# Gate 1 and shift 2 summed on VectorE during the scan, scale 2 and gate 2 on TensorE during convolution and gate

## The chip, the cores and the metric

The kernel runs on one core of a Trainium2 chip. The metric is the device time of one execution in microseconds (us); lower is better. Engines: PE is TensorE (PEld its weight loads), DVE is VectorE, ACT is ScalarE, POOL is GpSimd, SP is SyncE, whose queue issues nearly all transfers. Each engine works through its own instructions in a fixed order and waits for others by semaphores.

## The reference, cut to what matters

One layer works on 256 latent tokens `x` and 256 context tokens `ctx`, each 1024 wide. Six modulation vectors of 1024 come from the conditioning vector `c`:

```python
mod_x = (jax.nn.silu(c) @ w_mod[i] + b_mod[i]).reshape(b, N_MOD, 1, D_MODEL)
...
hx = modulate(rmsnorm(x, norm1_g[i]), mod_x[:, 0], mod_x[:, 1])
ox, _, _ = token_mixers(hx, *mix_w, conv_grid_cols, h0_f, h0_b)
x = x + mod_x[:, 2] * ox
x = x + mod_x[:, 5] * moe(modulate(rmsnorm(x, norm2_g[i]), mod_x[:, 3], mod_x[:, 4]), *moe_w)
return rmsnorm(x, final_g)
```

Vectors 0 and 1 (shift 1, scale 1) are wanted at once and are not touched here. Vector 2 (**gate 1**) is wanted after the out-projection, vectors 3 and 4 (**shift 2**, **scale 2**) ahead of the router, vector 5 (**gate 2**) in the mixture of experts. Each pair is a product of one row of 1024 with a 1024 x 2048 block of `w_mod` (8 MB), plus a bias.

`token_mixers` is an in-projection, a depthwise convolution, a bidirectional state-space scan over 16 heads, a second short convolution over three more slices of the projection (B, C, U), a SiLU gate z and an out-projection. `moe` is a top-4-of-32 mixture of experts, whose weights are some 400 MB.

## The kernel before

**Stages.** The program runs, in this order: modulation of shift 1 and scale 1 with the first projections; the decays (`token_steps`, `decay_rows`) and the x columns (`x_block`, `x_tokens`); the scan of 16 steps (`decays(s)`, then `outputs(s)`), in which blocks of the short convolution (`sc_block`) fill TensorE; the other 12 convolution blocks; eight gate blocks (`proj` of Z); the out-projection, in eight parts; the router; the experts.

**Order.** From L405 on, PE's order is that of the program text (`manual_schedule` for PE). The other engines' instructions and the transfers on SP's queue are put in order by a planner when the kernel is built; `tc.issue_after(i)` makes an instruction stand behind `i` on the same engine.

**The modulation products before.** `mods(1, ...)` is gate 1 with shift 2, `mods(2, ...)` scale 2 with gate 2. Each is a generator: eight steps k, and a last part. A step loads 1 MB of `w_mod` (`load_mod`, L187; two ring slots, `ringm`, so that step k+2 is loaded when step k has been read) and issues four matmuls (L202) of a 32-column stationary operand `ct[:, k, :]`, which the trace shows as eight. After step 7 the bias is added on DVE (L205). The last part (L209 to L218) turns one vector into columns (`pq`, 16 records) and spreads the other over all partitions (`pgate`, four records).

**Where the steps stand.** Three steps of `m1` stand between `c_block(0)` and `token_steps` (L649), two after `scores(1)` (L669), one in each scan step from 2 on (L679): `m1` to the end in steps 2 to 5, then `m2`, whose last part falls into step 14. One scan step before is: a convolution block of 24 matmuls, one step of `mods`, the decay matmuls `rb` of the next scan step, and the products `py` of this one. `decays` also makes six exponentials on ACT, two products `mx` on DVE (L586) and two `ex` on POOL (L588); `outputs` needs them one scan step later.

**Buffers the prediction speaks of.** `sacc` is one tile that `rows` of `m1`, `rows` of `m2` and then `bgr` (the rounded expert biases, L861 and L862) use in turn. The ring slot of `bg`, which `bgr` is made from, is later used by one of the eight loads `wo` of the out-projection. `proj` and `misc` are pairs of PSUM buffers. `hi` and `lo` (L287, L288) are the two parts into which each weight block is split, on ACT and on DVE or POOL.

Of the kernel before, what the change touches and what calls it, by code (L numbers as in the profile page):

```python
# [8 lines left out]
F32 = mybir.dt.float32  # L9
# [5 lines left out]
ALU = mybir.AluOpType  # L15
# [3 lines left out]
P = 128  # L19
D = 1024  # L20
KD = D // P
# [41 lines left out]
def body(ctx, tc, x, ctx_in, vectors_in, w_mod, b_mod, w_in, w_out, w_router, b_router, w_gate_up, b_gate_up,  # L63
         w_down, b_down, final_g, out, taps=None):
    nc = tc.nc
# [126 lines left out]
    def mods(ph, gate, gate_first, col):  # L192

        acc = ps.tile([P, 512], F32, tag="pm", bufs=1, name=f"pmod{ph}")
        rows = mp.tile([P, 512], F32, tag="sacc", name=f"rows{ph}")
        nc.gpsimd.memset(rows, 0.0)
        nc.gpsimd.dma_start(rows.rearrange("(j p) n -> j p n", p=32)[:, 0, :],
                            dram(b_mod, ph * 2048, [[512, 4], [1, 512]]))
        for k in range(KD):
            w = load_mod(ph, k)  # L200
            for j in range(4):
                nc.tensor.matmul(acc[32 * j:32 * j + 32, :], ct[:, k, :], w[:, 512 * j:512 * j + 512],  # L202
                                 start=(k == 0), stop=(k == KD - 1), skip_group_check=True)
            if k == KD - 1:
                nc.vector.tensor_add(rows, rows, acc)  # L205
            yield
        jg, jc = (0, 2) if gate_first else (2, 0)
        pq = ps.tile([P, 512], F32, tag="misc", bufs=2, name=f"pq{ph}")
        for q in range(KD):  # L209
            j = jc + q // 4  # L210
            nc.tensor.matmul(pq[:, q:q + 1], rows[:, (q % 4) * P:(q % 4 + 1) * P], ident[:, 32 * j:32 * j + 1],
                             start=True, stop=True)
        nc.vector.tensor_copy(col, pq[:, 0:KD])
        for hf in range(2):
            j = jg + hf
            pg = ps.tile([P, 512], F32, tag="misc", bufs=2, name=f"pgate{ph}_{hf}")
            nc.tensor.matmul(pg, ident[:, 32 * j:32 * j + 1].to_broadcast([P, P]), rows, start=True, stop=True)
            nc.scalar.copy(gate[:, hf, :], pg)  # L218
        yield

# [256 lines left out]
    sh2 = cn.tile([P, 8], F32, name="sh2")  # L477
    g1 = mp.tile([P, 2, 512], F32, tag="g1", name="g1")
    g2 = mp.tile([P, 2, 512], F32, name="g2")
    m1 = mods(1, g1, True, sh2)  # L480
    m2 = mods(2, g2, False, gs2)
    yb = mp.tile([P, 8, T], F32, tag="x28", name="yb")
    ws = t2a.tile([P, 2, NT, NH, HD], F32, tag="big8", name="ws")
# [66 lines left out]
    cb = [None, None]  # L550
# [14 lines left out]
    def decays(s_):  # L565

        hp, d_ = s_ // 2, s_ % 2
        g = hp // 4
        ja, jb = (0, 1) if d_ == 0 else (1, 0)
        mxs, exs = [], []  # L570
        for h_ in (2 * hp, 2 * hp + 1):
            row = 32 * d_ + h_
            pr = ps.tile([P, 4, P], F32, tag="rb", bufs=2, name=f"rb{h_}_{d_}")
            nc.tensor.matmul(pr, selr[:, row:row + 1].to_broadcast([P, P]), a4, start=True, stop=False,
                             skip_group_check=True)
            for blk in (0, 2) if d_ == 0 else (1, 2):
                nc.tensor.matmul(pr[:, blk, :], identb, maskf if d_ == 0 else maskb, start=False,
                                 stop=(blk == 2), skip_group_check=True)
            mx = t2s.tile([P, 384], F32, tag="mx", bufs=4, name=f"mx{h_}_{d_}")
            with tc.issue_after(last_silu):  # L580
                nc.scalar.activation(mx[:, 0:256], pr[:, 0:2, :].rearrange("p a b -> p (a b)"), AF.Exp,
                                     bias=dtc[:, 2, ja, row:row + 1])
                nc.scalar.activation(mx[:, 256:384], pr[:, 2, :], AF.Exp, bias=dtc[:, 2, jb, row:row + 1])
                ex = t2s.tile([P, 2, P], F32, tag="ex", bufs=4, name=f"ex{h_}_{d_}")
                nc.scalar.activation(ex, pr[:, 3:0:-2, :] if d_ == 0 else pr[:, 0:4:3, :], AF.Exp)
            nc.vector.tensor_mul(mx, mx, cb[g][d_])  # L586
            exf = ex.rearrange("p a b -> p (a b)")
            nc.gpsimd.tensor_tensor(exf, exf, cch[g], op=ALU.mult)  # L588
            mxs.append(mx)
            exs.append(exf)  # L590
        return mxs, exs
# [3 lines left out]
    def outputs(s_, mxs, exs):  # L595
        hp, d_ = s_ // 2, s_ % 2
        g = hp // 4
        ja, jb = (0, 1) if d_ == 0 else (1, 0)
        half = slice(P, T) if d_ == 0 else slice(0, P)
        xd = xdt[:, d_]  # L600
        if d_ == 0:
            py[0] = ps.tile([P, T], F32, tag="py", bufs=1, name=f"py{hp}")
        for hh in range(2):
            nc.tensor.matmul(py[0][64 * hh:64 * hh + 64, :], xd[:, ja, 2 * hp + hh, :], mxs[hh][:, 0:256],
                             start=(d_ == 0), stop=False, skip_group_check=True)
        for hh in range(2):
            nc.tensor.matmul(py[0][64 * hh:64 * hh + 64, half], xd[:, jb, 2 * hp + hh, :], mxs[hh][:, 256:384],
                             start=False, stop=False, skip_group_check=True)
        for hh in range(2):
            h_ = 2 * hp + hh  # L610
            nc.tensor.matmul(py[0][64 * hh:64 * hh + 64, :], h0[d_][g][:, (h_ % 8) * HD:(h_ % 8 + 1) * HD], exs[hh],
                             start=False, stop=(d_ == 1), skip_group_check=True)
        if d_ == 1:
            nc.vector.tensor_add(yb[:, hp, :], yb[:, hp, :], py[0])
# [31 lines left out]
    context_b(1)  # L646
    x_block(3)
    c_block(0)
    for _ in range(3):  # L649
        next(m1)  # L650
    token_steps()
    x_tokens(0)
    x_tokens(1)
# [12 lines left out]
    last_silu = x_block(7)  # L666
    x_tokens(6)
    scores(1)
    for _ in range(2):  # L669
        next(m1)  # L670
    x_tokens(7)
    sc_steps = [(kind, 2 * q + half) for q in range(4) for kind in "CUB" for half in range(2)]
    fill = [lambda: context_state(0, 1), lambda: context_state(1, 1)]
# [2 lines left out]
    for s_ in range(16):  # L676
        if fill:
            fill.pop(0)()
        if s_ >= 2:  # L679
            next(m1 if s_ < 6 else m2, None)  # L680
        done_ = step
        if s_ < 15:
            step = decays(s_ + 1)
        outputs(s_, *done_)
    tap("y", yb)
    sa.close()
# [8 lines left out]
    def sc_parts():  # L695
        while sc_done:
            ti, v_ = sc_done.pop(0)
            nc.scalar.copy(sc[0][:, ti, :], v_)
            nc.gpsimd.tensor_tensor(sc[1][:, ti, :], v_, sc[0][:, ti, :].bitcast(F32), op=ALU.subtract)

    sc_parts()
    for a in sc_steps[12:]:
        sc_block(*a)
        sc_parts()


    yhl = [scp.tile([P, 2, 4, T], F32R, tag=("ya", "yb")[g], name=f"y{g}") for g in range(2)]
# [56 lines left out]
    for q in range(4):  # L764
        if q == 3:
            wo0, slot0 = load_out(0), ring[-1]
            ahead = [row_parts(wo0, 0, hf, order[0]) for hf in range(2)]
        wv = load_cols(256 * q, f"Z{q}")
        for half in range(2):
            ti = 2 * q + half  # L770
            pp = proj(wv, half, T, f"Z{ti}", nc.vector)
            z = t2b.tile([P, T], F32, tag="cv1", bufs=6, name=f"z{ti}")
            nc.scalar.activation(z, pp[:, :T], AF.Silu)
            nc.vector.tensor_mul(yb[:, ti, :], yb[:, ti, :], z)
# [703 lines left out]
```

## Time and profile before

| | |
|---|---|
| median of 3 runs | 1302.51 us (1299.98 to 1302.81) |
| the profiled execution | 1297.97 us, of which the span is 1296.2 us |
| mean granted clock of TensorE | 0.97 of full speed |
| busy share of the span | PE 90%, DVE 34%, ACT 20%, POOL 9% |
| moved | 466.12 MB, mean 360 GB/s |

The span is the time from the first to the last instruction of the profiled execution; the 1.8 us beside it lie outside. Busy shares are averages over stages with different limits, so a stage has to be read by itself. A matmul's duration in a list of instructions overlaps its neighbours'; what a run of matmuls costs is read from the chain of work that ended last, or from the distance of two starts.

### The profile page before, as it was taken

Reading aid. Unit: us, or ns where it says so; the run is one execution under the profiler, and the core shown is the slowest. Engines: PE = TensorE matmul, PEld = TensorE weight load, DVE = VectorE, ACT = ScalarE, POOL = GpSimd, SP = SyncE. Lnnn points to the kernel's source line nnn. Section 1 sums busy time; section 2 is a strip of 40 time slices with the busy share of each in tenths; the row PEclk is TensorE's granted clock in tenths of the full one; section 3 lists DMA queues with packets and bytes.
Section 4 is the critical chain, followed back from the end, with each engine's and each line's share of the span. In section 5 each row is a group of like instructions: output and inputs, shape, how many; then the busy total and the mean of one; then the engine's idle time right before and its main releaser. Section 6 shows DMA issues by size and latency. Waiting matters only on the chain.

```text
span 1296.2 us, 16117 instructions
## 1 busy us (share of the span) xinstructions
PE 1170.4 (90%) x6113; PEld 538.1 (42%) x6113; DVE 435.6 (34%) x878; ACT 258.4 (20%) x510; POOL 122.1 (9%) x140
## 2 busy tenths in 40 slices
PE   7989999999899989899898878998977899888985
PEld 6666767988433322243222223422321243223221
DVE  5475454654432432213324212222321113212222
ACT  5444544554400010010001001000100010001002
POOL 1232333426100100000000000000000000000000
PEclk9999999999899999999999989999998999899998
DMA  9743468786499999999999999999999999999994
GB/s 324 266 164 130 164 228 280 257 294 270 170 417 415 416 415 417 416 416 417 417 416 416 416 416 416 416 416 416 416 416 417 417 416 417 416 416 416 416 415 186
DMA packets 111841, 466.12 MB, mean 360 GB/s; under 512 B 9576, under 2 KB 40424, under 8 KB 76944
## 3 DMA queue, kind: packets, MB, share of 16 engines
q1 hardware_dynamic: 111504, 464.37, 90.4%
q8 instruction: 50, 0.82, 0.3%
q0 software_dynamic: 256, 0.67, 0.1%
q14 instruction: 31, 0.25, 0.1%
HBM read 463.97 MB, written 1.05 MB: 359 GB/s over the span
## 4 chain that ended last, share of the span: by engine, by line
PE 77%; DMA 13%; DVE 6%; ACT 2%; issue 1%; SPq 1%; POOL 0%; ACTq 0%; DVEq 0%; POOLq 0%
PE pdn L1123 8%; PE pg L1111 8%; DMA gu<-in_w_gate_up_dram 8%; PE pl L1111 7%; PE pg L1191 6%; PE pc L1087 6%; PE pgl L1160 6%; PE pdn L1175 4%; PE pdn L1198 3%; DMA dn<-in_w_down_dram 3%; PE pd L999 2%; DMA wim<-in_w_mod_dram 2%; PE pgl L1154 1%; PE pat L1080 1%; PE ppX L293 1%; PE ppX L294 1%
## 5 line engine op out<-in xcount | busy, mean ns | idle before, releaser
L1111 PE MATMUL pg<-gu,xe 128*64 128x512 f32 x480 | 152.6, 610 | 1.5 <-DMA gu<-in_w_gate_up_dram 1.5
L1111 PE MATMUL pl<-gu,xe 128*64 128x512 f32 x480 | 149.3, 599 | 0.0
L1054 ACT ACTIVATE s<-a 128x512 f32<-128x512 f32 (+1 forms) x35 | 19.1, 545 | 591.0 <-DVE a L1053 591.0
L1087 PE MATMUL pc<-ye,gt 64*128 64x512 f32 (+1 forms) x248 | 100.3, 647 | 27.6 <-DVE ye L1134 14.5
L1160 PE MATMUL pgl<-gu,xe 128*32 128x512 f32 x896 | 114.4, 617 | 11.8 <-DMA gu<-in_w_gate_up_dram 11.8
L1123 PE MATMUL pdn<-dn,at 128*64 128x512 f32 x480 | 117.3, 634 | 6.9 <-ACT at L1082 6.8
L1089 DVE TENSOR_TENSOR x<-x,pc 128x512 f32<-128x512 f32 x124 | 81.7, 684 | 123.1 <-PE pc L1087 123.1
L1053 DVE TENSOR_SCALAR a<-pg 128x512 f32<-128x512 f32 x21 | 14.5, 690 | 216.0 <-PE pg L1111 150.5
L1191 PE MATMUL pg<-gu,xe 128*128 128x512 f32 x192 | 83.9, 592 | 0.0
L1134 DVE TENSOR_TENSOR ye<-g2s,pdn 128x512 f32<-128x512 f32 x29 | 19.9, 687 | 153.1 <-PE pdn L1123 106.3
L1313 POOL DMA_DIRECT2D fg<-in_final_g_dram x1 | 0.6, 591 | 746.4 <-PE pd L999 746.4
L1087 PEld LDWEIGHTS pc<-ye,gt 64*128 64x128 f32 (+1 forms) x248 | 28.5, 186 | 100.5 <-DVE x L1089 42.9
L1111 PEld LDWEIGHTS pl<-gu,xe 128*64 128x64 f32 x480 | 42.2, 138 | 67.1 <-issue 66.8
L1175 PE MATMUL pdn<-dn,at 128*32 128x512 f32 x448 | 63.4, 674 | 6.5 <-ACT at L1082 5.4
L1111 PEld LDWEIGHTS pg<-gu,xe 128*64 128x64 f32 x480 | 38.5, 138 | 69.9 <-issue 60.1
L1123 PEld LDWEIGHTS pdn<-dn,at 128*64 128x64 f32 x480 | 33.9, 145 | 72.8 <-issue 58.0
L1160 PEld LDWEIGHTS pgl<-gu,xe 128*32 128x32 f32 x896 | 24.9, 111 | 88.4 <-issue 56.7
L1191 PEld LDWEIGHTS pg<-gu,xe 128*128 128x128 f32 x192 | 35.8, 190 | 41.6 <-issue 40.9
L999 PE MATMUL pd<-oh,hr 128*128 128x256 f32 (+1 forms) x256 | 41.9, 305 | 5.6 <-DVE xe L1001 5.0
L1198 PE MATMUL pdn<-dn,at 128*128 128x512 f32 x96 | 43.5, 601 | 0.0
L999 PEld LDWEIGHTS pd<-oh,hr 128*128 128x128 f32 x256 | 34.2, 198 | 20.9 <-DVE xe L1001 10.7
L1067 DVE TENSOR_SCALAR go<-io,gp 128x128 f32<-128x128 f32 x56 | 18.6, 369 | 67.0 <-PE pgo L1071 67.0
(406 smaller groups left out, 1635.0 us busy)
## 6 DMA issues: line engine op xcount, KB each, us to landing
gu<-in_w_gate_up_dram SPq DMA_DIRECT2D x256, 1024.0 KB, 19.9
dn<-in_w_down_dram SPq DMA_DIRECT2D x127, 1024.0 KB, 20.0
wm<-in_w_mod_dram SPq DMA_DIRECT2D x16, 1024.0 KB, 5.2
wim<-in_w_mod_dram SPq DMA_DIRECT2D x8, 1024.0 KB, 11.6
wo<-in_w_out_dram SPq DMA_DIRECT2D x8, 1024.0 KB, 5.1
wiX<-in_w_in_dram SPq DMA_DIRECT2D x4, 1024.0 KB, 9.9
wiSC<-in_w_in_dram SPq DMA_DIRECT2D x4, 1024.0 KB, 6.4
wiSU<-in_w_in_dram SPq DMA_DIRECT2D x4, 1024.0 KB, 6.5
```

The lines of the kernel that those rows point to most:

```text
L999: nc.tensor.matmul(pd[:, :width], hr[n // 2][:, n % 2, k * P:(k + 1) * P], oh[:, n % 2, :], start=(n == 0), stop=(n == 3))
L1054: nc.scalar.activation(s, a, AF.Sigmoid, scale=ALPHA)
L1067: nc.vector.tensor_scalar(go if cap == P else go.rearrange("p (a s) -> p a s", s=cap), io1 if cap == P else io1[:, None, 0:cap].to_broadca ...
L1087: nc.tensor.matmul(pc_, lhs, rhs, start=True, stop=True)
L1089: return nc.vector.tensor_add(ysl, ysl, pc_).ins
L1111: nc.tensor.matmul(pp[64 * hf:64 * hf + 64, :], xk[k], gu[k][:, i * FF + hf * 512:i * FF + hf * 512 + 512], start=False, stop=(k == KD - 1 ...
L1123: down = nc.tensor.matmul(pdn[64 * hf:64 * hf + 64, :], at[:, kk % 4, 64 * (kk // 4):64 * (kk // 4) + 64], dn[kk // 2][:, (kk % 2) * D + h ...
L1134: nc.vector.tensor_mul(ye, g2s, pdn)
L1160: nc.tensor.matmul(pgl[32 * q:32 * q + 32, :], xk[k], gv[:, :, 256 * q:256 * q + 256], start=False, stop=(k == KD - 1), skip_group_check=True)
L1175: down = nc.tensor.matmul(pdn[j:j + 32, :], at[:, c2, 32 * q:32 * q + 32], dn[q][:, c2 * D + hf * 512:c2 * D + hf * 512 + 512], start=(q = ...
L1191: nc.tensor.matmul(pgs[i][hf], xk[k], gu[k][:, i * FF + hf * 512:i * FF + hf * 512 + 512], start=False, stop=(k == KD - 1))
L1198: nc.tensor.matmul(pdn, ats[kk // 4][:, kk % 4, :], dn[kk // 2][:, (kk % 2) * D + hf * 512:(kk % 2) * D + hf * 512 + 512], start=(kk == 0) ...
```

## The change

`m1` is made by a new generator, `mods_by_rows`; `m2` stays as it was. For each k, `mods_by_rows` multiplies the two halves of the loaded 128 x 2048 block by the per-partition scalar `ct[:, k, 0:1]` and adds them to two accumulators of 128 x 1024 (`gate`, `sacc`) with `scalar_tensor_tensor` on DVE: two instructions in a step, 16 in all, each pair ordered behind the last `mx` product that the program text has issued. GpSimd clears the accumulators and loads the biases into their first rows. The last part sums over the partitions with matmuls against ones: eight for the columns of shift 2, two for gate 1.

The places move: the three early steps and the two after `scores(1)` are gone; a step of `m1` stands in each odd scan step (1, 3, ... 15), behind `decays`; the last part of `m1` stands behind the first of the 12 later convolution blocks, steps 0 to 2 of `m2` behind the fourth, seventh and tenth, steps 3 to 7 behind the matmuls of gate blocks 0 to 4, and the last part of `m2` behind those of gate block 5.

```diff
+    scanned = [None]
+
+    def mods_by_rows(ph, gate, gate_first, col):
+        sacc = mp.tile([P, 2, 512], F32, tag="sacc", name=f"sacc{ph}")
+        parts = (gate, sacc) if gate_first else (sacc, gate)
+        for h_, a in enumerate(parts):
+            nc.gpsimd.memset(a, 0.0)
+            nc.gpsimd.dma_start(a[0:1], dram(b_mod, ph * 2048 + h_ * 1024, [[0, 1], [512, 2], [1, 512]]))
+        for k in range(KD):
+            w = load_mod(ph, k)
+            with tc.issue_after(scanned[0]):
+                for j in range(2):
+                    a = parts[j].rearrange("p a n -> p (a n)")
+                    nc.vector.scalar_tensor_tensor(a, w[:, D * j:D * j + D], ct[:, k, 0:1], a,
+                                                   op0=ALU.mult, op1=ALU.add)
+            yield
+        pq = ps.tile([P, 512], F32, tag="misc", bufs=2, name=f"pq{ph}")
+        for q in range(KD):
+            nc.tensor.matmul(pq[:, q:q + 1], sacc[:, q // 4, (q % 4) * P:(q % 4 + 1) * P], onesf[:, 0:1],
+                             start=True, stop=True)
+        nc.vector.tensor_copy(col, pq[:, 0:KD])
+        for hf in range(2):
+            pg = ps.tile([P, 512], F32, tag="misc", bufs=2, name=f"pgate{ph}_{hf}")
+            nc.tensor.matmul(pg, onesf, gate[:, hf, :], start=True, stop=True)
+            nc.scalar.copy(gate[:, hf, :], pg)
+        yield
...
-    m1 = mods(1, g1, True, sh2)
+    m1 = mods_by_rows(1, g1, True, sh2)
...
-            nc.vector.tensor_mul(mx, mx, cb[g][d_])
+            scanned[0] = nc.vector.tensor_mul(mx, mx, cb[g][d_]).ins
...
     c_block(0)
-    for _ in range(3):
-        next(m1)
     token_steps()
...
     scores(1)
-    for _ in range(2):
-        next(m1)
     x_tokens(7)
...
-        if s_ >= 2:
-            next(m1 if s_ < 6 else m2, None)
         done_ = step
         if s_ < 15:
             step = decays(s_ + 1)
+        if s_ % 2:
+            next(m1)
         outputs(s_, *done_)
...
-    for a in sc_steps[12:]:
+    for i_, a in enumerate(sc_steps[12:]):
         sc_block(*a)
         sc_parts()
+        if i_ % 3 == 0:
+            next(m2 if i_ else m1)
...
             pp = proj(wv, half, T, f"Z{ti}", nc.vector)
+            if ti < 6:
+                next(m2)
```

## Rows read from the trace of the kernel before

**Rows 1.** The page, part 2: GB/s moved in 40 slices of the span.

```profile
GB/s 324 266 164 130 164 228 280 257 294 270 170 417 415 416 415 417 416 416 417 417 416 416 416 416 416 416 416 416 416 416 417 417 416 417 416 416 416 416 415 186
```

**Rows 2.** Stretches: length, busy PE, PEld, DVE, ACT, POOL; granted clock, DMA share, GB/s.

```profile
75.57:83.83 8.26, 3.87 (x26) 0.69 (x26) 8.04 (x18) 3.94 (x5) 3.47 (x2) 0.88 0.70 256
...
131.84:217.26 85.42, 85.06 (x665) 59.25 (x663) 43.80 (x67) 42.27 (x104) 32.12 (x36) 1.00 0.66 221
...
217.26:251.86 34.60, 34.60 (x289) 34.60 (x289) 20.25 (x29) 15.77 (x21) 13.14 (x10) 1.00 0.78 254
251.86:274.94 23.08, 23.08 (x194) 23.08 (x193) 12.85 (x17) 11.64 (x17) 2.65 (x2) 1.00 0.70 237
274.94:321.90 46.96, 46.28 (x218) 37.90 (x217) 21.68 (x40) 24.50 (x48) 27.79 (x25) 1.00 0.79 311
321.90:346.00 24.10, 18.75 (x100) 12.33 (x100) 17.49 (x47) 12.66 (x32) 6.29 (x5) 0.86 0.27 102
400.00:1280.00 880.00, 786.62 (x3672) 266.22 (x3672) 227.60 (x456) 74.38 (x160) 5.58 (x5) 0.97 1.01 414
```

**Rows 3.** Waits of PE, whole span: us in total, times, longest.

```profile
PE pmod L202 <- DMA wm<-in_w_mod_dram: 4.4, 1, 4.4
...
PE px L519 <- DVE ws L522: 1.0, 1, 1.0
```

**Rows 4.** The chain that ended last, 70 to 90 us: start, us, what.

```profile
75.64 1.04 PE pmod L202 x8
...
76.70 5.14 DMA wm<-in_w_mod_dram
...
83.82 0.83 PE pc L470 x6
...
86.09 0.12 PE ppC L293
```

**Rows 5.** DVE's instructions in order of time, around 80 us.

```profile
76.44 0.40 DVE L460 TENSOR_TENSOR wc<-wc,dtx 64x256 f32<-64x256 f32 x1
...
79.52 3.25 DVE L288 TENSOR_TENSOR loC<-wiC,hiC 128x1024 fp32r<-128x1024 f32 x1
82.69 0.73 DVE L312 SCALAR_TENSOR_TENSOR cv<-ppX,vs,cv 128x510 f32<-128x510 f32 x1
```

**Rows 6.** ACT's instructions in order of time, around 79 us.

```profile
78.97 0.77 ACT L311 ACTIVATE cv<-ppX,vs 128x512 f32<-128x512 f32 x1
```

**Rows 7.** POOL's instructions in order of time, around 79 us.

```profile
79.23 2.46 POOL L288 TENSOR_TENSOR loX<-wiX,hiX 128x1024 fp32r<-128x1024 f32 x1
```

**Rows 8.** The chain that ended last, in the scan: start, us, what.

```profile
174.90 1.00 PE pmod L202 x8
...
176.86 0.58 PE py L604 x4
...
209.43 1.88 PE pq L211 x16
211.30 1.84 PE pgate L217 x4
...
215.31 0.67 DVE mx L586
```

**Rows 9.** Groups by form, 131.84 to 217.26 us: busy us, mean ns.

```profile
L202 PE MATMUL pmod<-wm,ct 128*32 128x512 f32 x88 | 11.7, 605 | 0.0
...
L288 DVE TENSOR_TENSOR loSC<-wiSC,hiSC 128x1024 fp32r<-128x1024 f32 x4 | 4.9, 1218 | 0.0
```

**Rows 10.** DVE's instructions in order of time, in the scan.

```profile
172.24 1.11 DVE L586 TENSOR_TENSOR mx<-mx,cbf 128x384 f32<-128x384 f32 x1
```

**Rows 11.** Groups by form, 60 to 80 us: busy us, mean ns.

```profile
L438 DVE SCALAR_TENSOR_TENSOR e<-e,e 64x512 f32<-64x512 f32 x1 | 0.7, 682 | 0.0
```

**Rows 12.** The tile of the `w_mod` loads: time from issue to landing.

```profile
DMA to landing us min/median/max: 4.7/5.2/8.4
```

**Rows 13.** Waits of SP's own queue.

```profile
SPq L751 <- DVE bgr L862: 2.4, 1, 2.4
```

## The prediction

> **What bounds the kernel now.** I read the page's slices first: from the twelfth on, the transfers run at 415 to 417 GB/s up to the last one [rows 1], and from 400 to 1280 us the share of the transfer engines is 1.01 [rows 2]. The experts are bound by transfers; the stretch ahead of them only decides when that stream can start. Its start is set by the first ring slot that the first expert gives back, for ahead of it the transfers stand idle: their share is 0.27 between 321.90 and 346 us, because every slot is full [rows 2]. So what the change saves or costs before the first expert moves the end by as much, as long as the slots are still full by then.
>
> The second view is busy time by stage [rows 2]. In the scan (131.84 to 217.26 us) PE works 85.06 of 85.42 us, in convolution and gate (to 274.94) all of the time. There each microsecond put on PE or taken off it counts in full. The one stretch where it doesn't is 75.57 to 83.83 us: PE 3.87 of 8.26 us, DVE 8.04.
>
> The third view is PE's waits: the longest in this part is the 4.4 us for the third `wm` block; later there is 1.0 us for `ws` [rows 3]. The scan has none worth naming. So the change lives or dies by how much PE work really disappears, and by whether DVE, which gets new work, makes PE wait.
>
> **Part 1: what only moves.** `m2`'s eight steps (1.00 us each [rows 8]) and its last part (1.88 + 1.84 = 3.72 us [rows 8]) go from the scan to convolution and gate, both full on PE: 0. The last part of `m1` moves likewise and keeps its size (eight column products and two of 512 columns with a 128-row operand, as before): 0. In all about 15.4 us leave the scan and come back behind it.
>
> **Part 2: three steps of `m1` that leave the scan.** 88 records [rows 9] are 11 steps of eight, eight of `m2` and three of `m1`: -3.0 us.
>
> **Part 3: three steps ahead of `token_steps`.** From the first `pmod` at 75.64 to `pc` at 83.82 are 8.2 us: two steps, the 5.14 us transfer that could only start when a slot was read, and the third step [rows 4]. But `pc` also needs `wc`, which DVE has only at 76.84 [rows 5], so 6.9 us at most come free. Nor can PE run on for all of that: the next projection, `ppC` at 86.09 [rows 4], needs the PSUM buffer that X block 3's two `cv` instructions on DVE release. ACT's part of it ended at 79.74 [rows 6], and with two instructions of 0.73 us [rows 5] DVE could release it at 81.2: 4.9 us sooner, less some 0.4 of hand-over, so -4.5 at best. If DVE keeps its order, with `loC` ahead of `cv` (79.52, 82.69 [rows 5]), it is released at 84.2: -1.5. DVE is full here [rows 2], and the `dtc`, `xdt` and `ws` work now competes with it earlier. I take the middle: -3.0 us, between -4.5 and -1.5.
>
> **Part 4: two steps after `scores(1)`.** PE does them and then still waits 1.0 us for `ws` [rows 3]. Without them it waits 2 us longer: 0, at best -1.9 us if DVE is put in another order.
>
> **Part 5: what DVE gets.** 16 instructions over 1024 columns. One of 512 columns with two SBUF inputs takes 0.68 us [rows 11], `loSC`, a two-input instruction of 1024, takes 1.22 [rows 9]; I take 1.22, so a pair is 2.44 us and the eight are 19.5 us. Do they fit? Without the `pmod`s the stretch of 85.42 us shrinks by 11.0 + 3.5 + 3.7 = 18.2 to 67.2 us; DVE's 43.8 us [rows 2], less 1.6 us of `rows` and small copies, plus seven pairs in it are 59.3: 88%. The delay allowed: the second `mx` of a step ended at 173.35 [rows 10], and its `py` starts at 176.86 [rows 8], 1.0 us sooner without `pmod`: 2.5 us of slack against a pair of 2.44, which moreover stands behind that `mx`, not ahead of it. Queued behind a pair are `lo`, `cs` and `scv` (who wait for two blocks yet) and the next `mx`. So in full steps I charge 0. At the end it is tighter: steps 14 and 15 have no convolution block, and the 3.72 us of `m2`'s last part covered the last `mx`, which ended at 215.98, 2.8 us after that part [rows 8]. Of the 3.72 us part will turn into waiting, and a pair may stand ahead of the last `mx`. Bounds 0 and 3.7; I take +1.5, since `rb` and `py` fill about half of it.
>
> **Part 6: transfers.** `m1`'s blocks are read every second scan step, so a slot is free some 21 us before its next use: 0. In the gate, steps 5 to 7 of `m2` need a block whose slot was freed two gate blocks before: 2 x (2.88 + 1.00) - 1.0 = 6.8 us (2.88 is 23.08 us over eight blocks [rows 2]). Landing took 4.7 to 8.4 us, median 5.2 [rows 12]: 0 at the median, 3 x 1.6 at the worst, and the share of the transfer engines there was 0.70 [rows 2]: +0.7, up to 4.8. A wait is added on SP too: a `wo` load waits for `bgr` [rows 13], which now waits for `sacc`, free only after gate block 5. Behind it on SP stand the later `wo` loads and the first expert blocks, some 5 MB and 2 MB late. The out-projection wants that `wo` about 15 us later, and idle share (0.21 of 47 us and 0.73 of 24 us, 27 us [rows 2]) holds the 18 us that 7 MB take at 400 GB/s. With `bgr`'s instructions falling into busier time: +0.3, up to 1.5.
>
> **The sum.** -3.0 (scan) - 3.0 (early) + 0 + 1.5 (tail) + 0.7 + 0.3 = -3.5 us. The profiled execution would go from 1297.97 to 1294.5 us; it lies 4.5 us under the median of the runs shown, so against that median I forecast 1302.5 - 3.5 = 1299.0 us. The ends: -3.0 - 4.5 - 1.9 = -9.4 (1293.1), and -3.0 - 1.5 + 3.7 + 4.8 + 1.5 = +5.5 (1308.0), the latter only if all three losses come together. A measurement of this kernel can tell about 0.2%, 2.6 us, from no change.
>
> **Rivals.**
> *No difference.* The early gain stays at its lower end and the late losses are middling: -3.0 - 1.5 + 2.5 + 1.5 + 0.5 = 0, 1302.5 us. For it speaks that DVE, not PE, is the full engine where the wait is removed. Or the loads of the gate come late: +4.8 in place of 0.7 is +0.6, 1303.1 us. Together 0.30.
>
> *Slower: PE waits for `mx` behind the pairs.* The planner may put a pair ahead of the next step's `mx`, and a pair need not take 2.44 us: `loC` took 3.25 us in place of 1.22 while POOL ran `loX` to 81.69 [rows 5, 7], and the `ex` products and `scv` run on POOL in every such step. The slack of 2.5 us is what decides: above it each further delay is PE's. If each of seven pairs overruns by one instruction, 1.22 us, that is +8.5: 1307.5 us. Against it: it has to happen in most steps, and average DVE load leaves 12%. 0.14.
>
> *Slower: the new instructions run at half rate.* Two SBUF inputs might be read in turns; then a pair is 2 x (0.15 + 2 x 1.07) = 4.6 us (1.07 us being 1024 columns at the step of 1.05 ns between 0.68 us at 512 and 1.22 at 1024 [rows 9, 11]), seven are 32 us, DVE has 74 us of work in 67, and the sum is -3.5 + 6.9 = +3.4: 1305.9 us. Against it: the 0.68 us instruction is just such a one and shows no second reading. The Trainium skill has this as a rule (Vector Engine (DVE) Microarchitecture Reference, "Points that are easy to get wrong"): a scalar-tensor-tensor instruction with two SBUF sources that aren't bf16 halves its throughput. The trace so far doesn't bear that out. 0.05.
>
> *The change doesn't do what it says.* The planner puts pairs off, past the scan, so that the last part of `m1` waits on PE behind the first convolution block: two pairs late are +4.9, 1303.9 to 1307 us. `issue_after` holds only one side of the order. 0.03.
>
> **How the numbers follow.** The forecast with its better variants (the early stretch at -4.5, the tail at 0) has 0.48; it needs the early gain to be over its lower end, which I can't see from here. No difference 0.30, slower 0.22. Its own range is 1293 to 1300. The range leaves out the end below 1293.5 and part of the slower cases, 0.05 and 0.13: 1293.5 to 1306.5.
>
> **What would show it.** In the trace after: no `pmod` before the scan, and `pc` near 77 in place of 83.8; `ppC` between 81.6 and 84.5 (part 3); scan steps with a convolution block 5.3 us apart in place of 6.3, with no PE wait for `mx` (parts 2, 5); pairs of 1.2 us each (2.3 would be the half-rate rival); gate blocks 3.9 us apart with no PE wait for `wm` (part 6); the transfers idle again before the first expert's slot is free. I am wrong if PE's waits for `mx` in the scan sum to over 4 us, if `ppC` starts no sooner than 85, or if the transfers no longer pause at about 330 to 345 us.

## The result: 0.98% slower, and where the time went

| | before | after |
|---|---|---|
| median | 1301.24 us (4 runs, 1298.65 to 1302.81) | 1312.74 us (4 runs, 1311.45 to 1315.43) |
| profiled execution, span | 1297.97 us, 1296.2 us | 1315.43 us, 1313.7 us |
| mean granted clock of TensorE | 0.97 | 0.949 |

The medians differ by 11.5 us (0.88%); the ratio over the runs is 1.0098 (95% interval 1.0081 to 1.0116). So some 12 us are lost, where I forecast 3.5 us won, and the time lies outside my range too. The profiled execution of after is the slowest of its four, that of before the fastest of its four, so the two traces differ by 17.5 us.

First, the stages of after, as stretches of the trace (length, busy PE, PEld, DVE, ACT, POOL; granted clock, DMA share, GB/s). The first five lines are the scan, the later convolution blocks, the gate, the out-projection, and the stretch in which the experts run; the last is the pause of the transfers ahead of the first expert.

```profile
135.20:216.81 81.61, 71.07 (x537) 56.46 (x535) 66.73 (x78) 40.12 (x100) 38.65 (x36) 0.90 0.54 171
216.81:258.90 42.09, 42.09 (x333) 38.22 (x333) 20.48 (x30) 16.81 (x23) 14.51 (x11) 0.99 0.86 286
258.90:291.40 32.50, 32.50 (x255) 26.68 (x254) 13.92 (x20) 13.01 (x19) 1.22 (x1) 1.00 0.85 314
291.40:337.40 46.00, 45.33 (x214) 37.10 (x213) 20.82 (x38) 24.50 (x48) 27.17 (x25) 1.00 0.80 311
415.00:1295.00 880.00, 795.45 (x3674) 268.77 (x3670) 227.76 (x456) 74.45 (x160) 5.57 (x5) 0.95 1.01 415
350.00:360.00 10.00, 8.31 (x39) 6.31 (x38) 6.28 (x19) 3.76 (x11) 0.00 (x0) 0.66 0.00 2
```

Against [rows 2]: the scan begins 3.4 us later (135.20 for 131.84) though 5 us of PE work ahead of it are gone. It is 81.6 us long, 3.8 us shorter than before, not 16.7. Convolution and gate take 74.6 us for 57.7, as their new work asks. From the out-projection on nothing has changed by more than about 1 us: the experts are still bound by transfers, which still pause first (350 to 360 us, nothing moved). So what was lost ahead of them moved the end.

Second, PE's waits from 70 to 290 us (us in total, times, longest):

```profile
PE py L632 <- DVE yb L642: 10.5, 4, 3.9
PE px L547 <- DVE dtc L501: 7.1, 1, 7.1
PE px L547 <- DVE ws L550: 2.8, 1, 2.8
```

Before there were 4.4 and 1.0 us [rows 3]. The 4.4 us for the `wm` block are gone; 7.1 us for `dtc` stand in their place. The 1.0 us have become 2.8, and 10.5 us are new in the scan.

**The early wait.** DVE, then PE, in order of time:

```profile
76.51 0.41 DVE L488 TENSOR_TENSOR wc<-wc,dtx 64x256 f32<-64x256 f32 x1
76.84 0.93 DVE L524 CAST a<-acs 32x128 fp32r<-32x128 f32 x5
77.80 1.76 DVE L526 TENSOR_TENSOR a<-acs,a 32x256 fp32r<-32x256 f32 x6
79.59 3.25 DVE L316 TENSOR_TENSOR loC<-wiC,hiC 128x1024 fp32r<-128x1024 f32 x1
82.77 0.74 DVE L340 SCALAR_TENSOR_TENSOR cv<-ppX,vs,cv 128x510 f32<-128x510 f32 x1
83.43 0.41 DVE L500 COPY dtc<-pc 128x256 f32<-128x256 f32 x1
...
84.80 0.27 DVE L501 TENSOR_SCALAR dtc<-pc 128x128 f32<-128x128 f32 x1
```

```profile
85.22 1.09 PE L547 MATMUL px<-ident,cx 128*128 128x128 f32 x4 [7.15 <-DVE dtc L501]
85.96 0.56 PE L321 MATMUL ppC<-hhi,hiC 128*128 128x256 f32 x1
```

PE had `pc` done at 77.4, as forecast. But ahead of the `dtc` copies that empty `pc`, DVE's order holds the decay rows (`a`, 2.7 us), `loC` (3.25 us) and `cv`. PE goes on at 85.22, and `ppC` starts at 85.96, where it started at 86.09 before [rows 4].

**The wait in the scan.** A pair and what follows it on DVE, then PE:

```profile
158.79 0.55 DVE L614 TENSOR_TENSOR mx<-mx,cbf 128x384 f32<-128x384 f32 x1
159.26 1.27 DVE L235 SCALAR_TENSOR_TENSOR g<-wm,ct,g 128x1024 f32<-128x1024 f32 x1
160.46 1.74 DVE L235 SCALAR_TENSOR_TENSOR sacc<-wm,ct,sacc 128x1024 f32<-128x1024 f32 x1
162.12 0.41 DVE L642 TENSOR_TENSOR yb<-yb,py 128x256 f32<-128x256 f32 x1
```

```profile
162.59 0.65 PE L632 MATMUL py<-mx,xdt 128*64 128x256 f32 x4 [3.06 <-DVE yb L642]
```

The next head pair's `mx` is there at 159.3. What PE waits for is the `yb` addition, which empties the one bank of `py`, and it stands behind the pair. That is so for five of the eight pairs; four of them make PE wait (3.1, 0.6, 3.0 and 3.9 us), and behind the last comes no further `py`. Ahead of the other three pairs the addition had already been done (it starts at 135.32, 145.48 and 181.34), and PE did not wait.

**The clock.** The granted clock (the number ahead of the DMA share; 0.50 is 1.2 GHz, 1.00 is 2.4) around and behind three of these waits, of 7.1, 2.8 and 3.1 us:

```profile
82.00:88.00 6.00, 2.78 (x13) 2.81 (x14) 6.00 (x15) 1.05 (x2) 2.50 (x2) 0.50 0.58 178
124.00:130.00 6.00, 5.97 (x17) 2.60 (x16) 2.83 (x7) 3.38 (x9) 1.91 (x2) 0.57 0.16 53
160.00:166.00 6.00, 3.42 (x20) 2.52 (x21) 4.93 (x7) 1.05 (x4) 2.54 (x2) 0.77 0.55 176
```

Behind these three waits PE works on at or near the lower level for several us; from 163 to 168 us, where it doesn't wait at all, the mean is 0.66. The first stretch was not at full clock before either, behind the 4.4 us wait for the `wm` block, which ended at 81.9:

```profile
82.00:88.00 6.00, 6.00 (x40) 4.08 (x41) 4.96 (x11) 1.72 (x3) 1.42 (x2) 0.73 0.94 318
```

From 124 to 130 us it was 1.00 before, and 1.00 in the scan [rows 2].

### The profile page after: what moved, and what is told of

Same layout as the page of the kernel before. It is cut to its first block, busy times and chain, and to the rows that moved or that the text cites. A ratio compares the mean times of both kernels' runs of the same rounds, so it can differ in the third digit from the quotient of the medians.

```text
span 1313.7 us, 16015 instructions
## 1 busy us (share of the span) xinstructions
PE 1181.2 (90%) x6049; PEld 546.3 (42%) x6049; DVE 459.9 (35%) x893; ACT 259.0 (20%) x510; POOL 131.4 (10%) x142
## 4 chain that ended last, share of the span: by engine, by line
PE 72%; DMA 11%; DVE 9%; issue 4%; ACT 2%; POOL 2%; SPq 1%; ACTq 0%; POOLq 0%; DVEq 0%
PE pdn L1151 8%; PE pg L1139 8%; PE pl L1139 7%; PE pc L1115 6%; PE pg L1219 6%; PE pgl L1188 6%; DMA gu<-in_w_gate_up_dram 5%; DMA dn<-in_w_down_dram 4%; PE pdn L1203 4%; PE pdn L1226 3%; PE pd L1027 2%; DMA wim<-in_w_mod_dram 2%; PE pgl L1182 1%; PE pat L1108 1%; DVE ye L1162 1%
## 5 line engine op out<-in xcount | busy, mean ns | idle before, releaser
L1115 PE MATMUL pc<-ye,gt 64*128 64x512 f32 (+1 forms) x248 | 103.2, 666 | 26.9 <-DVE ye L1162 14.6
L1117 DVE TENSOR_TENSOR x<-x,pc 128x512 f32<-128x512 f32 x124 | 81.6, 685 | 123.7 <-PE pc L1115 123.7
L1203 PE MATMUL pdn<-dn,at 128*32 128x512 f32 x448 | 67.8, 704 | 9.8 <-ACT at L1110 5.4
```

The source lines that it names most:

```text
L1115: nc.tensor.matmul(pc_, lhs, rhs, start=True, stop=True)
L1117: return nc.vector.tensor_add(ysl, ysl, pc_).ins
L1203: down = nc.tensor.matmul(pdn[j:j + 32, :], at[:, c2, 32 * q:32 * q + 32], dn[q][:, c2 * D + hf * 512:c2 * D + hf * 512 + 512], start=(q = ...
```

## The experiments

In each table, "first block" is the start of the first convolution block, "out-projection" that of its first product; times in us, ratios with their 95% intervals against the kernel before on the same chip (median 1298.9 to 1299.9 in the four sets). All start from the changed kernel but one, which says so. The changed kernel itself was measured only once, beside a before of 1301.24, so a difference to its 1312.74 us is uncertain by some 2 us; the kernel with two halves of `py`, which has the same waits, came to 1313.03 in one of the later sets.

| run | median | ratio | first block | out-projection | span |
|---|---|---|---|---|---|
| before | | 1 | 131.8 | 274.9 | 1296.2 |
| the change | 1312.74 | 1.0098 (1.0081 to 1.0116) | 135.2 | 291.4 | 1313.7 |
| pairs behind yb | 1304.67 | 1.0036 (1.0022 to 1.0050) | 134.6 | 281.8 | 1302.0 |
| early order | 1317.00 | 1.0134 (1.0117 to 1.0152) | 137.0 | 293.1 | 1315.2 |
| both orders | 1306.68 | 1.0051 (1.0034 to 1.0068) | 137.2 | 283.4 | 1305.1 |
| places alone | 1304.97 | 1.0040 (1.0025 to 1.0055) | 136.6 | 282.2 | 1304.6 |
| early cover | 1307.87 | 1.0073 (1.0055 to 1.0090) | 131.8 | 284.3 | 1306.9 |
| m2 early | 1290.99 | 0.9941 (0.9927 to 0.9956) | 132.5 | 268.2 | 1288.8 |
| m2 spread alone | 1300.85 | 1.0013 (1.0004 to 1.0022) | 131.8 | 275.6 | 1299.0 |
| two halves of py | 1313.03 | 1.0109 (1.0095 to 1.0124) | 134.2 | 289.6 | 1311.2 |
| py in two banks | 1304.43 | 1.0033 (1.0020 to 1.0047) | 136.4 | 282.1 | 1303.8 |
| decay rows late | 1308.53 | 1.0076 (1.0060 to 1.0091) | 133.0 | 284.1 | 1306.3 |
| m2 early, decay late | 1289.36 | 0.9932 (0.9918 to 0.9946) | 131.2 | 266.9 | 1287.5 |
| the change well ordered | 1297.12 | 0.9983 (0.9973 to 0.9993) | 131.1 | 273.7 | 1294.5 |

### Pairs behind yb

```diff
-            scanned[0] = nc.vector.tensor_mul(mx, mx, cb[g][d_]).ins
+            nc.vector.tensor_mul(mx, mx, cb[g][d_])
...
+            scanned[0] = nc.vector.tensor_add(yb[:, hp, :], yb[:, hp, :], py[0]).ins
...
-        if s_ % 2:
-            next(m1)
         outputs(s_, *done_)
+        if s_ % 2:
+            next(m1)
```

> The changed kernel with one order altered: a pair of VectorE's new instructions stands behind the addition to yb that empties the product buffer py in the same scan step, no longer behind the last mx product. Theory A (the pair stands ahead of that addition, py has one buffer, and the next step's py products wait; after each wait TensorE runs at 1.2 GHz for some microseconds): the four waits of 10.5 us in sum vanish, the granted clock stays 1.00 from 156 us to the end of the scan, the stretch from the first convolution block (135.2 us) to the fifth (216.8 us) shrinks from 81.6 to about 69 us, and the time falls by 10 to 13 us, to 1300 to 1303 us. Theory B (VectorE simply has too much work in the scan): the waits move to other instructions, mx above all, the stretch stays over 78 us and the time falls by less than 4 us.

PE's waits in the scan:

```profile
PE py L632 <- DVE yb L642: 2.3, 3, 1.9
PE py L632 <- DVE mx L614: 1.6, 1, 1.6
```

The waits for `yb` fell from 10.5 to 2.3 us and the time by 8.1 us, short of the 10 to 13 expected. What is left is nearly all at the end of the scan, where steps have no convolution block and are short. There DVE is late whichever way the pair stands (DVE, in order of time):

```profile
199.00 1.41 DVE L235 SCALAR_TENSOR_TENSOR g<-wm,ct,g 128x1024 f32<-128x1024 f32 x1
200.34 1.74 DVE L235 SCALAR_TENSOR_TENSOR sacc<-wm,ct,sacc 128x1024 f32<-128x1024 f32 x1
202.01 2.07 DVE L614 TENSOR_TENSOR mx<-mx,cbb 128x384 f32<-128x384 f32 x2
```

The last `mx` products stand behind a pair; the granted clock is 0.50 from 202 to 208 us.

### Early order, and both orders

```diff
+    with tc.issue_after(ws_done[0]):
+        decay_rows()
+    with tc.issue_after(dtc_done[0]):
+        c_block(1)
-    decay_rows()
-    c_block(1)
```

Here `dtc_done` is the second `dtc` copy and `ws_done` the last `ws` product of X block 1.

> The changed kernel with one order altered: on VectorE the decay rows stand behind the last product of the second token block (x_tokens(1)), and the second C block's part (lo) behind the copies into dtc. Theory A (with the three steps of shift 2 gone, TensorE reaches its transposes at 77 us but VectorE still does the decay rows and loC, 6.4 us, first; TensorE idles 7.1 us and then runs at 1.2 GHz): that wait falls under 2 us, X block 4 starts at about 86 in place of 90 us, and the time falls by 3 to 6 us, to 1307 to 1310 us. Theory B (VectorE is full in this stretch, so any order costs the same): X block 4 starts at 89 us or later and the time changes by less than 1.5 us.

> Both alterations of order together. If the two losses are separate (theory A of both): the time falls by their sum, 13 to 19 us, to 1294 to 1300 us, and that is 1 to 7 us under the kernel before, what the prediction had put on the change itself. If one of them covers the other (a gain early is waited away in the scan): no more than the larger of the two, 1300 us or over.

Worse by about 4 and 2 us than without this edit, which no theory had foreseen for the first. The wait had only moved (PE's waits of the first of the two):

```profile
PE ppC L324 <- DVE loC L316: 4.2, 1, 4.2
PE ppC L321 <- DVE cv L342: 2.8, 1, 2.8
```

I first took that for proof that DVE is full there in any order. The trace says less: this edit put `loC` last of all, behind the decay rows (DVE):

```profile
86.76 1.67 DVE L528 TENSOR_TENSOR a<-acs,a 32x256 fp32r<-32x256 f32 x6
88.47 1.22 DVE L316 TENSOR_TENSOR loC<-wiC,hiC 128x1024 fp32r<-128x1024 f32 x1
```

So the run on the decay rows alone, below, had to be made.

### Places alone

```diff
-    m1 = mods_by_rows(1, g1, True, sh2)
+    m1 = mods(1, g1, True, sh2)
```

> The places of the change alone: gate 1 and shift 2 are made on TensorE as before, eight steps of four matmuls, but in the places of the changed kernel (odd scan steps, and their last part behind the first later convolution block). Theory A (VectorE's pairs cost the scan some 13 us of waits, the empty places ahead of the scan 3 us or more): no wait for yb in the scan, its stretch from the first to the fifth convolution block about 75 us (seven steps of 1.0 us on top of 67.2), and the early wait of 7 us still there; the time is 1305 to 1309 us. Theory B (the loss comes from the places, above all from work moved into convolution and gate): within 2 us of the changed kernel, 1311 to 1315 us.

With all sixteen steps on PE, in the places of the change, the kernel is 7.8 us faster than the change: the scan has no PE wait, and its granted clock is 1.00. It is still 5.8 us over the kernel before. The five steps that stood early now stand where PE is full.

### Early cover

```diff
+    def keep_busy(n):
+        pk = ps.tile([P, 512], F32, tag="pm", bufs=1, name="pk")
+        for _ in range(n):
+            nc.tensor.matmul(pk[:, 0:P], ident, ident, start=True, stop=True)
...
     x_tokens(0)
+    keep_busy(24)
     x_tokens(1)
...
     scores(1)
+    keep_busy(9)
     x_tokens(7)
```

> The changed kernel plus products of the identity with itself on TensorE, whose result nobody reads: 24 between the tokens of X blocks 0 and 1 and 9 ahead of the tokens of X block 7, where TensorE now waits 7.1 and 2.8 us. No other edit. Theory A: the two waits belong to VectorE, but idling TensorE lowers the granted clock, and what follows runs at 0.50 for about 3 us (85 to 88) and 4.7 us (124 to 128.7); with the idle time filled the first convolution block starts 3 to 4 us sooner, at 131.3 to 132.3 in place of 135.2, and the time goes from 1312.7 to about 1309. Rival B: VectorE is full there and sets the pace at either clock; the first convolution block stays at 135 (within 1 us) and the time within 1.5 us of 1312.7.

Work that nobody needs made the kernel 4.9 us faster. DVE's order is that of the change and `px` starts no sooner (85.40), but the granted clock is 1.00 in both stretches (it was 0.73 and 0.72 over the same), and the first block starts at 131.8, 3.4 us sooner:

```profile
75.57:88.00 12.43, 9.58 (x83) 9.08 (x82) 12.24 (x30) 6.07 (x10) 6.28 (x4) 1.00 0.27 86
118.00:130.00 12.00, 10.51 (x63) 6.64 (x62) 8.00 (x17) 7.64 (x19) 4.43 (x5) 1.00 0.29 89
```

So what the first block lost against before, 3.4 us in these traces, is the clock; that it won nothing is left to explain (decay rows, below). The Trainium skill (TensorE: Matmul & The Clock Gate, "HAM oscillation — how this bites in real kernels") warns that gaps in TensorE's work bring its clock down in the middle of a kernel; this run agrees, with 3.4 us as the price of two gaps of 7.1 and 2.8 us beside the gaps themselves.

### Two halves of py, and py in two banks

```diff
+    py2 = ps.tile([P, 2, T], F32, tag="py", bufs=1, name="py2")
...
-            py[0] = ps.tile([P, T], F32, tag="py", bufs=1, name=f"py{hp}")
+            py[0] = py2[:, hp % 2]
```

> The changed kernel with the one PSUM bank of py used as two halves in turn, so that the products of the next head pair need not wait for the yb addition of the last one; places and order of the pairs as in the change. Theory A: what makes TensorE wait in the scan is the single py buffer, emptied by a yb addition that stands behind a pair: the 10.5 us of waits for yb fall to under 1, the granted clock stays at 1.00 from 136 to 205, the time falls to 1302 to 1305. Rival B: VectorE has too much to do there, and the wait goes over to mx: waits for yb and mx together stay over 6 us and the time within 3 us of 1312.7.

```profile
PE py L633 <- DVE yb L643: 10.5, 4, 3.9
```

Not a tenth of a microsecond was won, in the waits or in the time (1313.03 us, as rival B had it): as the program stands, two halves of one tile in one bank are one buffer. Whether the wait is for the tile or for the bank this run doesn't tell. The second try took another bank, which is free in the scan:

```diff
-            py[0] = ps.tile([P, T], F32, tag="py", bufs=1, name=f"py{hp}")
+            py[0] = ps.tile([P, 512], F32, tag=("py", "pm")[hp % 2], bufs=1, name=f"py{hp}")[:, :T]
```

> The changed kernel with py of odd head pairs in the PSUM bank that pmod uses later, so in two tiles of two banks; nothing else is altered. The kernel with two halves of one bank kept its 10.5 us of waits for yb, each as long as before, although the mx products had ended. Theory A: the wait is for the bank itself to be emptied by the yb addition behind the pair; with two banks the waits for yb in the scan fall under 3 us in sum and the time to 1303 to 1306, as with the pair put behind yb. Rival B: VectorE is too full in those steps, the waits turn into waits for mx of 6 us or more in sum, and the time stays over 1309.

```profile
PE py L632 <- DVE mx L614: 4.0, 3, 3.0
```

The wait for `yb` is gone without any pair being moved; 4.0 us for `mx` remain at the end of the scan, and the time fell by 8.3 us, as much as with the pairs behind `yb`. With that the cause in the scan is shown from two sides: one bank, emptied by an instruction behind the pair. The Trainium skill (PSUM — Partial Sum Buffer, "PSUM bank collisions raise a hardware error") asks for PSUM to be guarded by bank and quadrant (32 partitions), or more simply by bank, and not by address. The first of these two kernels waits as if guarded so; whether its halves could be used at once was not tried.

### Decay rows late

```diff
-    decay_rows()
     c_block(1)
     x_block(4)
     x_tokens(2)
     x_tokens(3)
+    with tc.issue_after(ws_done[0]):
+        decay_rows()
```

> The changed kernel with the decay rows on VectorE put behind the last product of x_tokens(3), and nothing held back for the second C block (its lo part then stands ahead of the wc product). Theory A: the early gain that the prediction counted on is there, and VectorE's order alone hid it: the tokens of X block 1 follow those of block 0 at once, the second C block starts at 81.5 to 82.5 in place of 86, the first convolution block at 130 to 131.5 in place of 135.2, and the time falls by 3.5 to 5 us to 1308 to 1309. Rival B: VectorE, ScalarE and GpSimd have enough to do between 76 and 92 us to set the pace in any order, as when both orders were tried together: first convolution block at 134.5 or later, time within 1.5 us of 1312.7.

```profile
81.66 0.55 PE L321 MATMUL ppC<-hhi,hiC 128*128 128x256 f32 x1 [1.87 <-DVE cv L342]
```

`ppC` starts at 81.66, 4.3 us sooner than after the change, and the time falls by 4.2 us. The first block gained only 2.2 us, less than expected: PE works on at a clock of 0.56 from 82 to 88 us, so that X block 4 starts at 86.92, 3.0 us sooner than after the change and 1.9 sooner than before; and the wait ahead of X block 7 stayed at 2.8 us and brought the clock down again (0.65 from 124 to 130 us). So an early gain was there; DVE's order hid it, not its load. What of the 4.2 us lies behind the first block isn't this gain: the waits there are the same, and only the clock differs (last section).

### m2 spread alone

This kernel is the one before with only `m2` in the places of the change.

```diff
-        if s_ >= 2:
-            next(m1 if s_ < 6 else m2, None)
+        if s_ >= 2:
+            next(m1, None)
...
+        if i_ and i_ % 3 == 0:
+            next(m2)
...
             pp = proj(wv, half, T, f"Z{ti}", nc.vector)
+            if ti < 6:
+                next(m2)
```

> The kernel before with m1 as it was (early steps, scan steps 2 to 5, all on TensorE) and only m2 moved to the places of the change: three steps behind the fourth, seventh and tenth later convolution block, five behind gate blocks 0 to 4, the last part behind gate block 5. Theory A: moving steps between places where TensorE is full costs nothing, and only the last scan steps lose cover: 1299 to 1301 against 1299.2, no wait of over 1 us for a block of w_mod. Rival B: the spread itself costs: 1303 or more, seen as gate blocks further apart than 2.88 plus 1.0 us by 0.2 us each and a wait at the end of the scan of over 2 us.

+1.95 us (0.13%, interval 0.04 to 0.22), a small loss inside the range of theory A, with 1.0 us of wait for `yb` at the end of the scan and none for `wm` in the gate.

### m2 early, and with the decay rows late

If early places are free, something should stand there. Here `m1` is on DVE as in the change, but five steps of `m2` take `m1`'s old early places; the pairs stand behind `yb` in scan steps 1 to 11 (odd), the last two behind the scan. Beside the edit of the pairs:

```diff
     c_block(0)
+    for _ in range(3):
+        next(m2)
     token_steps()
...
     scores(1)
+    for _ in range(2):
+        next(m2)
     x_tokens(7)
...
+        if s_ % 2 and s_ < 12:
+            next(m1)
+    for _ in range(2):
+        next(m1)
...
+        if i_ in (3, 6, 9):
+            next(m2 if i_ > 3 else m1)
...
+            if ti in (1, 3):
+                next(m2)
```

The tile `rows` of `m2` is made only at its step 5, since `m1` holds `sacc` until then.

> The pairs of m1 on VectorE behind each yb addition in scan steps 1, 3, 5, 7, 9 and 11, the last two behind the scan, the last part of m1 behind the fourth of the later convolution blocks; five steps of m2 in the early places that m1 had before (three ahead of the token steps, two behind scores(1)), the three others behind the seventh and tenth later block and the second gate block, the last part behind the fourth gate block. The whole reference is computed. Theory A: the early places cost TensorE nothing, every step elsewhere about 1.2 us, and pairs that stand behind yb and not in the last scan steps cost nothing: eight steps fewer than before on the paid places, -9.6 us, less about 2 us for the bare end of the scan: 1291.5 (1289 to 1296), first convolution block at 132. Rival B: a pair costs in waits what a step on TensorE costs, as the kernel with pairs behind yb (1304.7) was no faster than that with all steps on TensorE (1305.0): 1297 to 1301, with waits of over 4 us for yb or mx in the scan.

> The kernel with five early steps of m2 (1291.0) and with the decay rows late as in the run beside it; the third early step moves from ahead of the token steps to behind the second C block, so that the token steps wait for no transfer. The whole reference is computed. Theory A: the 4.2 us wait for the third block of w_mod goes, some 1.2 us of it come back as the step itself: first convolution block at 129.5 to 131 in place of 132.5, time 1288.5 to 1290. Rival B: the waits turn up again on VectorE's instructions: 132 or later, 1290.5 to 1293.

Both times came out inside their ranges: 0.59% and 0.68% faster than before. (The first block of the second, at 131.2, lies between the two theories.) In the second, the third early step moves behind `c_block(1)`, as its text says; the wait for the third `wm` block (4.2 us in the first) is gone, 3.0 us for `dtc` have taken its place, and of the scan's waits for `yb` 2.3 us are left (PE's waits):

```profile
PE px L550 <- DVE dtc L502: 3.0, 1, 3.0
PE py L635 <- DVE yb L645: 2.3, 3, 1.9
PE px L550 <- DVE ws L553: 1.0, 1, 1.0
```

### The change well ordered

The same work on the same engines as the change, without any early step, with three orders altered: decay rows late, pairs behind `yb`, the last two pairs behind the scan (and, to match, the last part of `m1` three blocks later, steps 0 and 1 of `m2` two and one block later).

> The change with three orders altered and the same work on the same engines: decay rows late; each pair behind the yb addition, in scan steps 1, 3, 5, 7, 9 and 11, the last two pairs behind the scan; the last part of m1 behind the fourth later convolution block, steps 0 to 2 of m2 behind the sixth, eighth and tenth; no step of m1 or m2 early. The whole reference is computed. Theory A (three separate losses that add): 1312.7 less 8.1 for the pairs behind yb, 4.2 for the decay rows and about 3 for the last pairs, 1297.5 (1295.5 to 1299.5): about the forecast of the prediction, and still 8 us above the kernel with five steps of m2 early (1289.4), since those five now stand on paid places (5 times 1.2) and the early waits are bare. Rival B: the losses share a cause and do not add: 1300 to 1305, or with waits of over 6 us left in the scan.

1297.12 us, where 1297.5 was expected. Of the 15.6 us gained, 8.1 are those of the run on the single `py` bank and 4.2 those of the run on the decay rows; the rest, 3.3, is left for the last pairs, near the 3 expected. That is a remainder: no run moved the last pairs alone, and 4.2 holds some of the clock's scatter. The trace agrees in kind: from 200 to 215 us the granted clock is 1.00, where it was 0.50 from 202 to 208 with the pairs behind `yb` alone. Beside the kernel with five steps of `m2` early and the decay rows late, its first block starts at the same time (131.1 and 131.2 us) although that kernel has five steps more ahead of it; the whole is 7.8 us longer. That shows it plainest: early, the steps are free, within the 2 us by which first blocks of like kernels differ (last section); five steps where PE is full would be 6 us.

## Why the prediction was wrong, step by step

**What bounds the kernel** held. PE is the bound from the scan to the gate, transfers from the experts on, and the pause between them is still there.

**Part 1 (moves, 0)** nearly held: +1.95 us for moving all of `m2`, by a run of its own, of which 1.0 is a new wait at the end of the scan. **Part 2 (-3.0)** had the right mechanism and was somewhat small: a step costs more than its 1.00 us, because the first matmul behind it takes 0.31 us in place of 0.12. The chain of after, in the gate:

```profile
261.98 1.00 PE pmod L202 x8
262.97 0.31 PE ppZ L321
263.29 0.12 PE ppZ L322
```

So three steps are 3.6 us, and gate blocks with a step stand 4.06 us apart where I had 3.88.

**Part 3 (-3.0, between -4.5 and -1.5) is the first step that failed**: it was +1.1, by the start of X block 4, the stage behind this place (before, then after):

```profile
88.79 0.40 PE L293 MATMUL ppX<-hhi,hiX 128*128 128x512 f32 x1
```

```profile
89.89 0.40 PE L321 MATMUL ppX<-hhi,hiX 128*128 128x512 f32 x1
```

I checked when `wc` and X block 3's `cv` let PE go on, but not when `dtc` does, which is the next thing that PE needs once `pc` stands at 77; DVE's order held 8 us of other work ahead of it. I had seen `loC` there and left the decay rows out. And I bounded the outcome at -1.5, as if work that is taken away could at worst save nothing. The removed steps had filled PE's wait: without them the wait was longer and the clock fell further, to 0.50 where it had been 0.73. With the wait covered X block 4 starts at 88.74, as before. The second of my three signs of error, `ppC` no sooner than 85, was met (85.96). The other half of the part was right: with the decay rows late PE waits for X block 3's `cv`, as I wrote, and `ppC` starts at 81.66, the best end of my range; but the clock left 1.9 of the 4.4 us at X block 4.

**Part 4 (0)** saw the wait grow from 1.0 to 2.8, as I wrote, but not the clock of 0.57 behind it. The tokens of X block 7, behind that wait, start 1.1 us later than before (123.06 for 121.94), the first convolution block 3.4 later: 2.2 us arise here, at a place that I had charged with nothing. The cover run gives both parts of the 3.4 us back.

**Part 5 (0 in full steps, +1.5 at the end) is the second step that failed**, and the larger: the scan shrank by 3.8 us where I had 16.7. Undisturbed, scan steps with a convolution block are 5.1 us apart (143.24, 148.32 and 153.40), a little under the 5.3 that I forecast. But four times PE waited for `yb`, 10.5 us in all. I listed what queues behind a pair as `lo`, `cs`, `scv` and the next `mx`, and left out `yb`. It comes once in two steps, and the next head pair's `py` can't start without it, since `py` has one bank. My slack of 2.5 us was that of `mx`. In the case shown above, `py` was full at 155.7 and wanted empty at 159.5 (the ends of the last `py` and of `rb` on PE); but the `mx` products stand ahead of the addition up to 159.3, so any pair between them and it is PE's in full. The slower rival had the right kind of loss (PE behind the pairs, +8.5 us) and the wrong instruction, at 0.14. The tail of +1.5 was some 3.3 us, by the remainder in the last run. A pair itself was close: 1.27 us for an instruction by itself, up to 1.76 when POOL works at the same time, against my 1.22.

**Part 6 (+0.7 and +0.3)** came out at its lower end: no wait for `wm` in the gate, the out-projection no longer than before (46.0 us for 47.0).

**The rival at half rate** fell. The instruction of 1024 columns takes 1.27 us where it takes least, as at 159.26 above, and 1.74 at 160.46 beside POOL; the medians of the two accumulators are 1.27 and 1.51. That is about twice the 0.68 us of 512 columns [rows 11], not four times. The rule of the Trainium skill that I cited with it (Vector Engine (DVE) Microarchitecture Reference, "Points that are easy to get wrong") doesn't show in this case: 1.27 us is near the 1.22 of the two-input `loSC` [rows 9].

**The sum.** With the three orders right the change gains 2.7 us (0.17%, interval 0.07 to 0.27), near the 3.5 that I forecast. That is in part luck, for its terms are others: in the traces the first block starts 0.8 us sooner than before where I had 3.0, and from there to the out-projection it takes 0.4 us less (142.7 for 143.1) where I had 0.8. The arithmetic of the removed work was sound; what it lacked was DVE's queue, instruction by instruction, at two places, and the clock.

## What to carry to other kernels

Before work is put on an engine that "has room", list everything in that engine's order that will stand behind it, and for each the buffer that it frees and who waits for that buffer; a busy share of 82%, as DVE's in the scan after (66.73 of 81.61 us), says nothing on this. Work that stands in another engine's wait is free and can be worth more than nothing, because TensorE keeps its clock (here 4.9 us for 33 matmuls that nobody needs): fill such places with useful steps first, and move to VectorE what stands where TensorE is full. An order given as "behind this" holds only one side, so read what stands in front of the instruction that the next stage needs.

## What the runs showed of the hardware that I had not expected

The clock's price for the same wait is not fixed. Five traces here (the change, pairs behind `yb`, places alone, two halves, two banks) have the same early waits, of 7.1 to 7.2 and 2.8 us; their first block starts between 134.2 and 136.6 us, so that the 3.4 us of the cover run is one value between 2.4 and 4.8. The changed kernel and the one with early cover have the same four waits in the scan (10.5 us), and nearly as many PE records from the first block to the gate, but differ in PE's busy time by 3.6 us and in granted clock (first line after, second with cover):

```profile
135.20:258.90 123.70, 113.16 (x868) 94.67 (x867) 87.22 (x107) 56.93 (x123) 53.16 (x46) 0.93 0.65 210
```

```profile
131.80:251.90 120.10, 109.57 (x868) 91.95 (x867) 87.22 (x107) 56.82 (x123) 53.16 (x46) 0.97 0.66 216
```

With the decay rows late the same stretch took 118.7 us (133.0 to 251.7), again with 10.5 us of waits. What makes the difference of up to 5 us between these traces stays open. It is a reason not to read a gain of a few us from two profiles alone: the medians put the cover's gain at 4.9 us, the two spans at 6.8.

Two DVE inputs from SBUF are slowed by POOL: 1.74 in place of 1.27 us for the new instruction, as 3.25 in place of 1.22 for `loC` [rows 5, 9]. Of the 16 new instructions the ten at 1.27 us ran without POOL or had begun ahead of its instruction (one of them, at 208.96, 0.1 us ahead); the six at 1.74 to 1.76 began while POOL worked. So a price taken by itself is a lower bound where POOL has work.
